# Softmax over 16,384 rows: tiles of twelve rows a partition in four buffers, instead of eight rows in six

## The chip, the cores and the metric

The kernel runs on one core of one Trainium2 chip. The metric is the device time of one execution in microseconds (us); for the kernel before it is the median of five runs. The engines named in the text are VectorE (DVE), ScalarE (ACT), SyncE (SP, which only issues loads here) and the core's 16 DMA engines, which move data between the chip's main memory (HBM) and the on-chip memory (SBUF, 128 partitions).

## The reference

A softmax with a temperature over the last axis of a 32 x 512 x 1024 array of float32 (64 MiB in, 64 MiB out):

```python
def reference(x, temperature):          # temperature = 0.5
    scaled = x / temperature
    shifted = scaled - np.max(scaled, axis=-1, keepdims=True)
    exp_x = np.exp(shifted)
    return (exp_x / np.sum(exp_x, axis=-1, keepdims=True)).astype(np.float32)
```

Each of the 16,384 rows of 1024 elements is independent of the others.

## The kernel before

The rows are cut into 16 tiles. A tile has eight neighbouring rows in each of 128 partitions, so a partition's share is 8 x 4 KiB = 32 KiB that lie in one piece in HBM and in SBUF, and the tile is 4 MiB. `TILES` (L10) lists the rows a partition of each tile, and `BUFS` (L11) says how many tiles' buffers there are: six, 192 KiB a partition. All work on a tile is done in place.

`load` (L57) issues one transfer of a whole tile on SP's queue. `store` (L97) issues one transfer of a whole tile on ACT's queue, and then calls `load` for the next tile that has not been loaded. That load goes into the buffer whose store was the oldest, and SP waits until that store has landed before it issues it (L61).

Inside a tile the rows are worked on in groups of four (`GROUP`, L13). For each group:

- `maximum` (L64): one VectorE reduction over 128 x 4 x 1024 elements (L70, the rows' maxima), and one tiny VectorE multiplication that makes the bias (L73).
- `exponential` (L75): four ScalarE activations (L79), one a row, which compute exp(scale * x + bias) in place and the row's sum beside it.
- `divide` (L88): one tiny VectorE reciprocal of the four sums (L91) and four VectorE multiplications (L93), one a row.

The order is written out by hand, with the scheduler of the language switched off. First `BUFS` loads are issued. Then a loop goes over the groups of all tiles; in each step comes the maximum and the exponential of group g, and then the division and the store of group g-1:

```python
for g in range(len(groups) + 1):
    if g < len(groups):
        maximum(g)
        exponential(g)
    if g > 0:
        divide(g - 1)
        store(g - 1)      # issues something only after a tile's last group
```

So the last division of a tile, and with it its store, stands on VectorE behind the first maximum of the next tile, which waits for that tile's load.

Of the kernel before, what the change touches and what calls it, by code (L numbers as in the profile page):

```python
# [1 line left out]

# [4 lines left out]

TILES = [[8]] * 16  # L10
BUFS = 6  # L11

GROUP = 4  # L13


@with_exitstack
def kernel(
    ctx: ExitStack,
    tc: tile.TileContext,
    x: bass.AP,  # L20
    temperature: bass.AP,
    out: bass.AP,
):
    nc = tc.nc
    f32 = mybir.dt.float32
    scale = 1.0 / float(temperature)
    extreme = mybir.AluOpType.max if scale > 0 else mybir.AluOpType.min

    P = 128
    xf = x.flatten_outer_dims()  # L30
    of = out.flatten_outer_dims()
    n, d = xf.shape
    assert sum(sum(ks) for ks in TILES) * P == n

    data = ctx.enter_context(tc.tile_pool(name="data", bufs=BUFS))
    stats = ctx.enter_context(tc.tile_pool(name="stats", bufs=4))


    groups, first, r = [], [], 0
    for i, ks in enumerate(TILES):  # L40
        first.append(r)
        r += sum(ks)
        a = 0
        for k in ks:
            for b in range(0, k, GROUP):
                m = min(GROUP, k - b)
                groups.append((i, a + b, m, (a, k) if b + m == k else None))
            a += k

    def dram(t, i):  # L50
        k = sum(TILES[i])
        block = t[P * first[i] : P * (first[i] + k), :]
        return block.rearrange("(p k) d -> p k d", p=P, k=k)

    tiles, small = [], []

    def load():  # L57
        i = len(tiles)
        if i < len(TILES):
            xt = data.tile([P, sum(TILES[i]), d], f32, name="xt")  # L60
            nc.sync.dma_start(out=xt, in_=dram(xf, i))  # L61
            tiles.append(xt)

    def maximum(g):  # L64
        i, a, k, _ = groups[g]
        top, bias, sums, recip = (
            stats.tile([P, k], f32, name=name) for name in ("top", "bias", "sums", "recip")
        )
        small.append((bias, sums, recip))
        nc.vector.tensor_reduce(  # L70
            out=top, in_=tiles[i][:, a : a + k, :], axis=mybir.AxisListType.X, op=extreme
        )
        nc.vector.tensor_scalar_mul(bias, in0=top, scalar1=-scale)  # L73

    def exponential(g):  # L75
        i, a, k, _ = groups[g]
        bias, sums, _ = small[g]
        for b in range(k):
            nc.scalar.activation(  # L79
                tiles[i][:, a + b, :],  # L80
                tiles[i][:, a + b, :],
                mybir.ActivationFunctionType.Exp,
                bias=bias[:, b : b + 1],
                scale=scale,
                accum_out=sums[:, b : b + 1],
            )

    def divide(g):  # L88
        i, a, k, _ = groups[g]
        _, sums, recip = small[g]  # L90
        nc.vector.reciprocal(recip, sums)  # L91
        for b in range(k):
            nc.vector.tensor_scalar_mul(  # L93
                tiles[i][:, a + b, :], in0=tiles[i][:, a + b, :], scalar1=recip[:, b : b + 1]
            )

    def store(g):  # L97
        i, _, _, part = groups[g]
        if part:
            a, k = part  # L100
            nc.scalar.dma_start(out=dram(of, i)[:, a : a + k, :], in_=tiles[i][:, a : a + k, :])
            if a + k == sum(TILES[i]):
                load()

    with tc.manual_schedule():
        for _ in range(BUFS):
            load()
# [6 lines that stand above are left out]
                store(g - 1)  # L116


# [1 line left out]
_INS = ['x', 'temperature']  # L120
_OUTS = [((32, 512, 1024), 'float32')]

_NUMBERS = {'temperature': 0.5}


# [26 lines left out]
```

## Time and profile before

| what | value |
|---|---|
| median of 5 runs | 318.04 us (317.62 to 318.44) |
| the profiled execution | 317.94 us |
| its span, first to last instruction | 316.1 us |
| VectorE busy | 235.5 us (75%) |
| ScalarE busy | 149.6 us (47%) |
| moved by DMA | 134.25 MB, 425 GB/s over the span |
| loads: 16 of 4096 KB | 50.1 us from issue to landing (median) |
| stores: 16 of 4096 KB | 38.7 us from issue to landing (median) |

The profile is of one execution. The span is what its trace covers; the time of the execution has 1.8 us more around it. A transfer's time to landing contains the time that it stands behind others in its queue. The share of the DMA engines is the mean over 16 engines.

### The profile page before, as it was taken

How to read it: one execution, taken by the hardware profiler on the slowest of the kernel's cores; microseconds unless marked ns; L12 is line 12 of the kernel's file. 1: busy time of each engine (PE TensorE's matmuls, PEld its weight loads, DVE VectorE, ACT ScalarE, POOL GpSimd, SP SyncE). 2: the span in 40 equal slices, each digit the busy share in tenths (PEclk: the TensorE clock that was granted, in tenths of full speed). 3: DMA queues.
4: the chain of work that ended last, by engine and by line, in shares of the span. 5: the costliest groups of instructions: out<-in, count | busy, mean ns of one | idle time of the engine just before them, and what ended most of it. 6: DMA issues, size and time to landing. Idle time of an engine off the chain costs nothing.

```text
span 316.1 us, 620 instructions
## 1 busy us (share of the span) xinstructions
DVE 235.5 (75%) x224; ACT 149.6 (47%) x257; POOL 0.2 (0%) x4
## 2 busy tenths in 40 slices
DVE  0399999999689494994949859497693976949720
ACT  0176666666526255361554606556064560645500
POOL 0000000000000000000000000000000000000000
DMA  8999999999999999999999999999999999999996
GB/s 332 398 464 415 382 460 423 440 429 435 444 419 448 415 452 411 452 415 452 411 452 411 453 423 444 427 435 444 419 448 416 448 415 448 415 452 411 452 411 274
DMA packets 4612, 134.25 MB, mean 425 GB/s; under 512 B 512, under 2 KB 512, under 8 KB 512
## 3 DMA queue, kind: packets, MB, share of 16 engines
q1 hardware_dynamic: 2304, 67.11, 49.6%
q10 hardware_dynamic: 2304, 67.11, 49.2%
q14 instruction: 4, 0.03, 0.0%
HBM read 67.11 MB, written 67.11 MB: 425 GB/s over the span
## 4 chain that ended last, share of the span: by engine, by line
DVE 49%; DMA 32%; another core or an unknown queue 9%; ACT 5%; issue 1%; DVEq 0%; SPq 0%
DVE top L70 29%; DMA xt<-in_x_dram 20%; DVE xt L93 18%; DMA out_dram<-xt 12%; ACT xt L79 5%; DVE recip L91 1%; DVE bias L73 1%; DVEq L147 0%; SPq L61 0%
## 5 line engine op out<-in xcount | busy, mean ns | idle before, releaser
L79 ACT ACTIVATE xt<-xt,bias 128x1024 f32<-128x1024 f32 x128 | 145.4, 1137 | 136.7 <-DVE recip L91 119.4
L70 DVE TENSOR_REDUCE top<-xt 128x4 f32<-128x4096 f32 x32 | 141.3, 4416 | 62.6 <-DMA xt<-in_x_dram 62.6
L93 DVE TENSOR_SCALAR xt<-xt,recip 128x1024 f32<-128x1024 f32 x128 | 87.7, 750 | 1.1
L79 ACT ACTIVATION_READ_ACCUMULATOR xt<-xt,bias 128x1 f32 x128 | 23.9, 186 | 0.0
L79 ACT ACT_TABLE_LOAD x1 | 1.3, 1283 | 13.1 <-DMA xt<-in_x_dram 13.1
L91 DVE RECIPROCAL recip<-sums 128x4 f32<-128x4 f32 x32 | 5.5, 171 | 2.1 <-ACT xt L79 2.1
L73 DVE TENSOR_SCALAR bias<-top 128x4 f32<-128x4 f32 x32 | 5.5, 170 | 1.1
L133 POOL MEMSET const-uint8-127<- 128x1 uint8 x1 | 0.1, 103 | 0.0
L133 POOL MEMSET const-bfloat16-1.0<- 128x1 bf16 x1 | 0.1, 102 | 0.0
L133 POOL MEMSET const-float32-0.0<- 128x1 f32 x1 | 0.1, 99 | 0.2 <-issue 0.2
L133 POOL MEMSET const-float32-1.0<- 128x1 f32 x1 | 0.1, 99 | 0.0
## 6 DMA issues: line engine op xcount, KB each, us to landing
xt<-in_x_dram SPq DMA_DIRECT2D x16, 4096.0 KB, 50.1
out_dram<-xt ACTq DMA_DIRECT2D x16, 4096.0 KB, 38.7
```

The lines of the kernel that those rows point to most:

```text
L70: nc.vector.tensor_reduce(out=top, in_=tiles[i][:, a : a + k, :], axis=mybir.AxisListType.X, op=extreme)
L73: nc.vector.tensor_scalar_mul(bias, in0=top, scalar1=-scale)
L79: nc.scalar.activation(tiles[i][:, a + b, :], tiles[i][:, a + b, :], mybir.ActivationFunctionType.Exp, bias=bias[:, b : b + 1], scale=scal ...
L91: nc.vector.reciprocal(recip, sums)
L93: nc.vector.tensor_scalar_mul(tiles[i][:, a + b, :], in0=tiles[i][:, a + b, :], scalar1=recip[:, b : b + 1])
L133: nc = _bacc.Bacc("TRN2", target_bir_lowering=False, num_devices=1)
```

## The change

Ten tiles of twelve rows a partition (48 KiB a partition, 6 MiB a tile) and one of eight rows (4 MiB) take the place of 16 tiles of eight rows, and four buffers take the place of six. A buffer has the size of the largest tile, so the buffers take 192 KiB a partition as before. The groups of four rows stay: a tile of twelve has three groups, the last tile two. The loop and the order in it are not touched.

```diff
-TILES = [[8]] * 16
-BUFS = 6
+TILES = [[12]] * 10 + [[8]]
+BUFS = 4
```

## The prediction

> **What bounds the kernel now.** I read the page's busy shares and slices first, then its queue lines, then the windows at the start, the middle and the end, then the waits, and last the timeline around the first and the last store. The page first:
>
> ```profile
> DVE 235.5 (75%) x224; ACT 149.6 (47%) x257; POOL 0.2 (0%) x4
> DMA  8999999999999999999999999999999999999996
> DMA packets 4612, 134.25 MB, mean 425 GB/s; under 512 B 512, under 2 KB 512, under 8 KB 512
> q1 hardware_dynamic: 2304, 67.11, 49.6%
> q10 hardware_dynamic: 2304, 67.11, 49.2%
> ```
>
> VectorE is idle a quarter of the span, ScalarE half; the DMA engines are full in every slice but the first and last. The two queues (q1 loads, q10 stores) together occupy 98.8% of 16 engines. Each has 2304 packets; 512 of all packets are tiny (one completion packet for each of 16 engines and 32 transfers), so 2048 of each queue are data: 67.11 MB / 2048 = 32,768 bytes, one partition's eight rows. The windows (start and end, then busy us with instructions of DVE, ACT, POOL, then clock, DMA share, GB/s) show where the engines are not full:
>
> ```profile
> 0.00:8.00 8.00, 0.00 (x0) 0.00 (x0) 0.20 (x4) 1.00 0.84 328
> 33.00:60.00 27.00, 26.72 (x25) 15.95 (x29) 0.00 (x0) 1.00 0.98 413
> 120.00:200.00 80.00, 61.22 (x60) 39.40 (x69) 0.00 (x0) 1.00 1.00 433
> 290.00:302.00 12.00, 9.99 (x13) 6.66 (x12) 0.00 (x0) 1.00 1.01 437
> 302.00:310.00 8.00, 0.41 (x1) 0.00 (x0) 0.00 (x0) 1.00 1.04 446
> 310.00:316.00 6.00, 0.00 (x0) 0.00 (x0) 0.00 (x0) 1.00 0.47 202
> ```
>
> Nothing is lost between about 2 us and 313 us, neither with loads alone (before 33 us), nor mixed, nor with stores alone. So the limit is the transfer work itself, and the waits agree: both computing engines and the load queue wait, in the end, for transfers.
>
> ```profile
> DVE top L70 <- DMA xt<-in_x_dram: 62.6, 12, 13.1
> SPq L61 <- DMA out_dram<-xt: 224.5, 10, 53.8
> ```
>
> The timeline gives the distances that decide whether the engines stay full (start, us, instruction):
>
> ```profile
> 13.07 4.42 DVE L70 TENSOR_REDUCE top<-xt 128x4 f32<-128x4096 f32 x1 [13.07 <-DMA xt<-in_x_dram]
> ...
> 32.78 0.38 ACTq L101 DMA_DIRECT2D out_dram<-xt  x1
> ...
> 282.68 4.42 DVE L70 TENSOR_REDUCE top<-xt 128x4 f32<-128x4096 f32 x1 [4.49 <-DMA xt<-in_x_dram]
> ...
> 290.19 0.34 ACTq L101 DMA_DIRECT2D out_dram<-xt  x1
> ...
> 302.44 0.34 ACTq L101 DMA_DIRECT2D out_dram<-xt  x1
> ```
>
> A tile's store leaves 7.5 us after the next tile lands (282.68 to 290.19), because its last division stands behind the next tile's first maximum; the last store leaves 19.8 us after the last landing. The packet records show the next-to-last store ending at 304.5 us and the last one's first packet at 303.3 us: the end is covered, by 1.2 us.
>
> **The change, part by part.** *Bytes* do not change: 134.2 MB. *Instructions* of VectorE and ScalarE do not change: 128 rows in groups of four are still 32 groups; of the issues, SP's and ACT's fall from 16 to 11 each. *Buffers*: 6 x 32 KiB and 4 x 48 KiB are both 192 KiB a partition.
>
> *Packets.* In the records a 32,768-byte packet starts 1,209.4 ns after the one before it, a 4-byte one 5.9 ns. (Two mixed rounds in the trace say the same: loads are seen to land 19.37 us apart, 204.58 to 223.95 on VectorE, and 16 x 1.209 + 2 x 0.006 = 19.36.) The line through the two has 27.22 bytes per ns and 5.7 ns for a packet as such. A 49,152-byte packet is then 1,805.7 + 5.7 = 1,811.4 ns. No row has that size, so two bounds: with no cost per packet it is 1.5 x 1,209.4 = 1,814.1 ns (saving nothing), and with all that the 4-byte packet shows, 1,811.2 ns. I take 1,811.4, since both rows lie on that line by construction and 4-byte packets are nearly all overhead.
> Per engine before: 16 tiles x 2 directions x 8 packets = 256 x 1.2094 + 32 x 0.006 = 309.80 us. After: 160 x 1.8114 + 16 x 1.2094 + 22 x 0.006 = 289.82 + 19.35 + 0.13 = 309.30 us. Saved: 0.5 us; bounds 0.1 (completion packets alone) and 0.5. Nothing in the trace excludes that a longer packet is slower per byte; that would be a loss, and the first rival prices its likeliest form.
> The Trainium skill, "DMA: Bandwidth & Descriptors", section "Why small descriptors are slow (HBM only)", gives a packet about 3 fixed cycles beside its 32-byte beats; by it a 32 KiB packet is 1024 + 3 cycles, and losing a third of them would be worth an estimated 0.3 us. The same page, section "SWDGE vs HWDGE vs iDMA", speaks against the change: a packet is the boundary at which an engine switches between queues, preferably at most 4096 bytes; here 32 KiB pieces already move as one packet at 433 GB/s in the mixed window, so no cost of it is seen.
>
> *Start.* The first transfer is half as long again: its first packet comes at 1.7 us as before, its landing at 13.05 + 8 x 0.602 = 17.9 us. The first store goes from after the second group to after the third: 32.78 - 13.05 = 19.7 us after landing, plus one group's step of 7.39 us (L70 starts at 32.66 and 40.05), so 45.0 us, 12.2 us later. The cover: 24 MiB of loads are in flight in both kernels, 4 x (8 x 1.811) = 58.0 us of work, ending alone at 60.5 us (0.75 us of first-packet latency included). By the packet records the first store's first packet came at 37.1 us, 4.3 us after its issue; again so, 49.3 us. 11.2 us of load work remains: covered, cost nothing. If that cover were gone, each us later would cost one.
>
> *Middle.* From 49.3 us both queues alternate. Loads end at 49.3 + 2 x 11.2 = 71.7; store 0 at 75.0, landing at 75.4 and releasing load 4 on SP, whose first packet (0.9 us after issue, as at 302.44) is at 76.4. For those 4.7 us no load is queued, but store 1 has been since 45.0 + 22.2 = 67.2 us. After that a load and a store of twelve rows take 29.0 us; load 4 lands near 105.8, load 9 at 250.8, VectorE needs 22.2 of each 29.0. Store to load release overlaps: store 1 lands at 103.0, the load before ends at 105.4.
>
> *End.* Load 10 is small: its eight 1.21 us packets alternate with 1.81 us ones, 24.2 us, landing at 275.0. Store 8 was issued at 250.8 + 7.5 = 258.3, store 9 at 282.5, store 10 at 275.0 + 19.8 = 294.8. Counted back from an end of work at 314.4 us: store 10 takes 9.7 us alone, store 9 14.5, so 9 begins near 290.2 and 10 near 304.7: each is queued some 8 to 10 us before its turn. No gap, cost nothing.
>
> *Sum.* The profiled execution took 317.94 us (span 316.1 and 1.8 around it), 0.1 under the median of 318.04. 317.94 - 0.5 = 317.44 (317.9 by the other bound), or 318.04 - 0.5 = 317.54 from the median; I take **317.5 us**.
>
> **The rivals.**
> *The pieces are cut.* If 48 KiB does not go as one packet, the change does not do what it says. As 32 + 16 KiB it is 16 packets a tile and direction: 336 an engine, 80 more than now, + 0.46 us: 318.4. As 16 KiB, 496: + 240 x 5.7 ns = 1.4, 319.3. Against: 32 KiB is seen whole. For: nothing larger is seen.
> *The shift at the start reaches the end (slower).* One mechanism: both rings run dry once because the first store is late, after which the 4.8 us later start is never caught up: 317.94 - 0.5 + 4.8 = 322.2. Place: between 45 and 76 us. It decides only if the first store's first packet comes after 60.5 us instead of 49.3; or if store 1 is issued after 75.0 instead of 67.2. For: the chain of waits of now begins with the landing and VectorE's unbroken work. Against: 62.6 us of VectorE's waiting for loads, which absorbs a late start.
> *The last engine.* By the records the engines' last packets end between 313.0 and 313.8 us, except two at 314.2 and 314.9, which each carried two instruction-fetch packets (8,192 bytes, 0.3 to 0.6 us of delay each). If those fall otherwise, up to 1.1 us more goes: 316.4.
>
> **How the numbers follow.** Forecast 0.68: its own range 316.9 to 318.1 (the saving between nothing and 0.5, and half a us either way for the last engine). What a measurement here can tell from no change is about 0.2%, 0.64 us, so faster means under 317.40: half of this case, 0.34 faster and 0.34 same. Last engine 0.11, faster. Cut pieces 0.07: 0.02 same, 0.05 slower. Shift 0.14, slower. Faster 0.45, same 0.36, slower 0.19. The range 316.4 to 319.0 takes in the forecast, the last engine and the milder cut, and leaves out the shift and the finer cuts, under 0.2.
>
> **What would show it.** Right: 1584 packets in each queue (11 transfers of 128 data and 16 completion packets), slices at 9 throughout, first store near 45 us, last near 295, DMA share of 0.99 or more in every window from 10 to 310 us. Wrong: more than 1584 packets in a queue (cut pieces); a window under 0.95 around 45 to 76 us or 280 to 305 us (shift, or an end that is not covered); a mixed rate under 430 GB/s, which no step here foresees.

## The result, and the profile after

The changed kernel takes **320.04 us** (median of 21 runs, 318.10 to 323.05); the kernel before took 318.01 us beside it (41 runs, 317.62 to 318.99). The ratio is 1.0055, 95% interval 1.0041 to 1.0069: slower by half a per cent, outside the forecast's range and on the other side of no change. As striking as the median is the spread: 5 us where the kernel before has 1.4. The ratios in this document leave out runs over 1.5% above the fastest of the same kernel, here the one of 323.05 us from which the first profile is, so for kernels with a wide spread they come out low. A second profile is read below, of a run of 319.96 us with a span of 317.9; the five runs taken with it were 319.96 to 320.81.

The page's slices and queue lines of that second profile:

```profile
DVE 235.1 (74%) x224; ACT 149.6 (47%) x257; POOL 0.2 (0%) x4
DMA  8999999999999999999999999999999999997997
DMA packets 3172, 134.25 MB, mean 422 GB/s; under 512 B 352, under 2 KB 352, under 8 KB 352
q1 hardware_dynamic: 1584, 67.11, 49.4%
q10 hardware_dynamic: 1584, 67.11, 48.8%
```

There are 1584 packets in each queue, as foreseen: the pieces are not cut. But with fewer packets and the same bytes, the two queues' share of a span that is 1.8 us longer has hardly fallen: 98.2% of 317.9 is 312.2 us, where 98.8% of 316.1 was 312.3. The work that should have become 0.5 us less did not. And a slice near the end shows a 7. The windows (start and end, busy us with instructions of DVE, ACT, POOL, clock, DMA share, GB/s):

```profile
33.00:60.00 27.00, 26.72 (x28) 16.36 (x29) 0.00 (x0) 1.00 1.02 433
60.00:90.00 30.00, 29.72 (x30) 19.01 (x33) 0.00 (x0) 1.00 0.98 422
120.00:200.00 80.00, 58.78 (x57) 39.02 (x68) 0.00 (x0) 1.00 1.00 432
282.00:290.00 8.00, 6.20 (x6) 2.89 (x7) 0.00 (x0) 1.00 0.77 332
290.00:302.00 12.00, 9.99 (x12) 7.71 (x14) 0.00 (x0) 1.00 0.92 397
302.00:310.00 8.00, 1.46 (x3) 0.00 (x0) 0.00 (x0) 1.00 0.91 393
```

The mixed middle runs at 432 GB/s, as before; then engines stand idle from 282 to 310 us, where the forecast had every transfer queued 8 to 10 us ahead. Two of the signs that it named for being wrong are here: an end that is not covered (0.77 and 0.92) and a mixed rate under 430 GB/s (422 from 60 to 90 us). The share needs care, since the kernel before has a window under 0.95 in the same place, although no engine has a gap there in its records:

```profile
282.00:290.00 8.00, 7.25 (x7) 2.61 (x5) 0.00 (x0) 1.00 0.94 406
```

The timeline (start, us, instruction; the issues of loads 4 and 5 are merged into one line) shows the late landing behind it:

```profile
45.57 0.38 ACTq L101 DMA_DIRECT2D out_dram<-xt  x1
...
78.26 25.66 SPq L61 DMA_DIRECT2D xt<-in_x_dram  x2
...
283.73 4.42 DVE L70 TENSOR_REDUCE top<-xt 128x4 f32<-128x4096 f32 x1 [2.28 <-DMA xt<-in_x_dram]
...
291.24 0.34 ACTq L101 DMA_DIRECT2D out_dram<-xt  x1
...
303.49 0.34 ACTq L101 DMA_DIRECT2D out_dram<-xt  x1
```

The last load landed at 283.7 instead of 275.0, so store 9 left at 291.2 instead of 282.5. The packet records say why. Of the 16 engines, 14 had finished their share of that load between 277.4 and 278.5 us; the last two at 280.8 and 281.6. The Trainium skill, "DMA: Bandwidth & Descriptors", section "Why a DMA increments its semaphore by 16 and not by 1", says that only the full count of all engines tells of a landing; this trace agrees, with the landing behind the last engine: its data ended at 281.6, its completion packet came behind one more store packet, at 283.4, and VectorE started at 283.7. Twelve engines ended store 8 near 288.5 and then stood idle for 3.2 to 3.9 us.

What delays an engine can be summed from the records. They do not name the engine; a packet is given to the engine whose packet before it ends as it starts, and the number of packets that each engine has of each transfer decides between several. The sums are good to some 0.3 us, and whether it is the same engine in every run is not known. A 32 KiB packet usually takes 1,213 ns, one of 48 KiB 1,815 (packets overlap by 3 to 4 ns, which gives the steps of 1,209 and 1,812). Call what a packet takes beyond the usual time of its length a *stall*, and sum stalls over each engine, without its first packet:

```
stalls per engine, us       largest   second   median engine
before                        1.7       1.5        0.7
changed, first profile        7.0       5.4        0.8
changed, second profile       4.0       3.3        0.8
```

The median engine is as it was. Single engines are not. Their stalls are nearly all on load packets, up to 1.1 us each, they are other sums in each run, and they set in at 48 us, when the first store's packets come between the loads.

These sums give the times. In all three profiles the engine that ends last has no gap, or 0.2 us of one, between its first packet and its last, while the others of the changed kernel stand idle for up to 3.9 us (second profile) and 6.8 us (first). So its own work is what the kernel takes. With 0.5 us less of packets the second profile should be 4.0 - 1.7 - 0.5 = 1.8 us longer than the one before, and the first 7.0 - 1.7 - 0.5 = 4.8; the spans are 1.8 and 4.9 us longer (317.9 and 321.0 against 316.1).

Instruction fetches alone do not explain a late engine. The two late engines of the second profile and the latest of the first each carried two of them (0.3 us each), but the second engine of the first profile (5.4 us) carried none, nor did the latest with the tiles in another order (4.7) and with short exponentials (8.6), two runs further down.

### The profile page after: what moved, and what is told of

It is laid out like the page before. It is cut to its first block, busy times and chain, and to the rows that moved or that the text cites. A ratio compares the mean times of both kernels' runs of the same rounds, so it can differ in the third digit from the quotient of the medians.

```text
span 321.0 us, 600 instructions
## 1 busy us (share of the span) xinstructions
DVE 235.1 (73%) x224; ACT 149.6 (47%) x257; POOL 0.2 (0%) x4
## 3 DMA queue, kind: packets, MB, share of 16 engines
q1 hardware_dynamic: 1584, 67.11, 48.9%
q10 hardware_dynamic: 1584, 67.11, 48.4%
## 4 chain that ended last, share of the span: by engine, by line
DMA 65%; DVE 23%; ACT 6%; issue 1%; DVEq 0%; SPq 0%
DMA xt<-in_x_dram 41%; DMA out_dram<-xt 24%; DVE top L70 15%; DVE xt L93 7%; ACT xt L79 6%; DVE bias L73 0%; DVE recip L91 0%; DVEq L147 0%; SPq L61 0%
## 5 line engine op out<-in xcount | busy, mean ns | idle before, releaser
L79 ACT ACTIVATE xt<-xt,bias 128x1024 f32<-128x1024 f32 x128 | 145.4, 1137 | 135.4 <-DVE recip L91 120.8
L79 ACT ACTIVATION_READ_ACCUMULATOR xt<-xt,bias 128x1 f32 x128 | 23.9, 186 | 0.0
```

Of the source, the lines that this page charges most:

```text
L79: nc.scalar.activation(tiles[i][:, a + b, :], tiles[i][:, a + b, :], mybir.ActivationFunctionType.Exp, bias=bias[:, b : b + 1], scale=scal ...
```

## The experiments

Three theories to begin with: *long packets* stall; a *step* of 48 KiB in the address from partition to partition makes engines collide; or the stalls were always there, and *fewer transfers* in fewer buffers no longer absorb them. All kernels below are edits of the changed kernel; each ratio is to the kernel before, run on the same chip.

**The changed kernel again** (no edit).

> The changed kernel once more, for a second profile. In the first one 14 of the 16 DMA engines followed the forecast (their share of the last load ended at 273.7 to 274.3 us) and two did not (281.2 and 284.3 us), because packets of 1.81 us took up to 1.6 us longer on those two, mostly loads. Three theories for these stalls. Long packets: pieces of 48 KiB stall where 32 KiB do not. Address step: a step of 48 KiB from partition to partition makes engines collide in the memory where 32 KiB does not. Fewer transfers: the stalls are always there, but with 11 transfers in four buffers each landing waits for the slowest engine and nothing absorbs it. All three: about 320 us, spread over 318 to 323; the time follows the slowest engine's sum of stalls, 1 us of it at 318.3 and 5 us at 322. Only fewer transfers: stalls no larger than the 2 us of the kernel before.

320.10 us (319.96 to 320.81), ratio 1.0073 (1.0061 to 1.0086). Stalls of 4.0 and 3.3 us on two engines, against 1.7 before: the stalls are larger than before, not only less well absorbed.

**Pieces cut in half, everything else kept.**

```diff
-            nc.sync.dma_start(out=xt, in_=dram(xf, i))
+            h = sum(TILES[i]) // 2
+            for b in (h, 0):
+                nc.sync.dma_start(out=xt[:, b : b + h, :], in_=dram(xf, i)[:, b : b + h, :])
...
-            nc.scalar.dma_start(out=dram(of, i)[:, a : a + k, :], in_=tiles[i][:, a : a + k, :])
+            h = k // 2
+            for b in (a, a + h):
+                nc.scalar.dma_start(out=dram(of, i)[:, b : b + h, :], in_=tiles[i][:, b : b + h, :])
```

> Each tile is loaded and stored in two transfers of half its rows (24 KiB pieces at a step of 48 KiB; the second half is loaded first, so that the first group still waits for the whole tile). Tiles, buffers and order as in the changed kernel; 336 packets an engine, some 0.9 us of packet cost more than with 171. Long packets: stalls gone, 318.4 (318.0 to 318.9), spread under 1 us. Address step and fewer transfers: 319.5 to 321, spread of 3 us or more, one or two engines with 3 to 6 us of stalls.

318.86 us (318.70 to 319.02), ratio 1.0027 (1.0016 to 1.0037). The spread falls to 0.3 us and the largest stall sum to 2.0. The same tiles, buffers, order and address step, so neither the step nor the tile size makes the stalls. The last tile is cut too, which makes 352 packets an engine instead of the 336 expected. The remaining 0.9 us over the kernel before is more than the 0.5 that 96 more packets cost; the rest was not taken apart.

**Tiles of six rows in eight buffers** (`TILES = [[6]] * 21 + [[2]]`, `BUFS = 8`).

> 21 tiles of six rows and one of two, in eight buffers (192 KiB as before): pieces of 24 KiB at a step of 24 KiB, which like 48 KiB is no power of two. 344 packets an engine, 0.5 us of packet cost more than the kernel before. Long packets and fewer transfers: 318.5 (318.1 to 319.0), little spread. Address step: stalls on single engines, 319.5 to 321, spread of 3 us.

318.51 us (318.37 to 318.86), ratio 1.0018 (1.0009 to 1.0027); largest stall sum 1.9. The forecast's price of a packet holds here: 96 more of them than in the kernel before (352, not the 344 expected), at 5.7 ns + 0.5 us, and 0.5 us measured.

**The kernel before with five buffers** (`TILES = [[8]] * 16`, `BUFS = 5`).

> The kernel before with five buffers instead of six (160 KiB): one transfer less in reserve, pieces of 32 KiB as before. Long packets and address step: 317.8 to 318.4, the same as before, since the load queue of the kernel before has 19 us in reserve and loses one tile of it. Fewer transfers: slower and spread, 318.8 to 320.

317.85 us (317.69 to 318.40), ratio 0.9996 (0.9988 to 1.0005): no difference. A transfer less in reserve costs nothing while no engine is late.

Long packets are left. The next runs ask how a late engine turns into time, and which packets must be long.

**Store 9 no longer waits for load 10.**

```diff
         for g in range(len(groups) + 1):
+            early = g == len(groups) - 2
+            if early:
+                divide(g - 1)
+                store(g - 1)
             if g < len(groups):
                 maximum(g)
                 exponential(g)
-            if g > 0:
+            if g > 0 and not early:
```

> The changed kernel with one thing moved: ahead of the last tile's first maximum come the last division and the store of the tile before it, so that store 9 no longer waits for the landing of load 10. In the second profile of the changed kernel 12 of 16 DMA engines stood idle for 3.2 to 3.9 us from 288.4 us on, since store 9 was issued 7.5 us after load 10 had landed, and that landing waited for the engines with stalls; those engines themselves stood idle for 0.4 to 1.1 us only. Stalls and late store together: the gap closes, and the slowest engine's own work is left: 318.9 (318.3 to 319.5). Stalls alone: 320.1, unchanged. Late store alone: 317.3.

319.48 us (318.14 to 321.91), ratio 1.0052 (1.0028 to 1.0077): not to be told from the changed kernel. Its profile, of a run of 318.15 us, shows store 9 at 284.45 and the end filled (timeline, then windows):

```profile
284.45 0.34 ACTq L101 DMA_DIRECT2D out_dram<-xt  x1
```

```profile
282.00:290.00 8.00, 7.96 (x7) 0.96 (x1) 0.00 (x0) 1.00 0.98 424
290.00:302.00 12.00, 9.28 (x12) 8.21 (x16) 0.00 (x0) 1.00 1.02 442
```

But the spread of the times stays. The profiled run is one of the three fastest of the twelve, with a largest stall sum of 2.9 us; no longer run of this kernel was profiled. In the changed kernel the idle time at the end was that of engines that waited for the late ones. How much of the median the gap itself costs is not settled: the last store still waits for the last landing, and the expected 318.9 lies within what was seen.

**Ten rows, and ten rows with the same move** (`TILES = [[10]] * 12 + [[8]]`; the second with the edit above).

> Twelve tiles of ten rows and one of eight in four buffers: 40 KiB pieces, 208 packets an engine, 0.3 us of packet cost less than the kernel before. If stalls grow with the length of a piece: one or two engines with 2 to 4 us, 318.6 (318.0 to 319.3). If they begin only above 40 KiB: 317.7 (317.4 to 318.1). If they begin right above 32 KiB: 319 to 320.5 as with twelve rows.

> Tiles of ten rows, with the store of the last large tile moved ahead of the last tile's first maximum. With ten rows no engine had stalls over 2 us, but engines stood idle for 1 to 1.8 us from 291.3 us on, waiting for the store that followed the last landing. If that late store is the whole loss of ten rows: 317.2 (316.9 to 317.7), the packet saving of 0.3 us and a little more, faster than both kernels. If a kernel of this length ends with its transfer work anyway, the gap only moves: 318.3, unchanged.

318.34 us (318.21 to 318.83), ratio 1.0010 (1.0001 to 1.0019); with the move 318.42 (318.05 to 318.63), ratio 1.0010 (1.0002 to 1.0019). Both were to be faster than this by one theory or another. (The groups in a tile of ten are of four, four and two rows, which gives VectorE 242 instructions instead of 224.) The windows of the two profiles, without and with the move:

```profile
290.00:302.00 12.00, 9.92 (x14) 9.28 (x16) 0.00 (x0) 1.00 0.85 365
```

```profile
290.00:302.00 12.00, 10.09 (x12) 9.10 (x16) 0.00 (x0) 1.00 0.99 427
```

The move fills the end (0.85 to 0.99) and the time stays: in the first the engines all end at 314.9 to 315.0 us, in the second between 313.0 and 315.1. The slowest engine sets the end, and a gap on the others costs nothing: without the move two engines had no gap at all. At 40 KiB the largest stall sums are 2.3 and 2.5 us, each on an engine that carried two instruction fetches, and the eleven times of each kernel lie within 0.7 us.

**Eleven rows** (`TILES = [[11]] * 11 + [[7]]`, 44 KiB).

> Eleven tiles of eleven rows and one of seven in four buffers: 44 KiB pieces, 190 packets an engine. Ten rows took 318.2 to 318.8 without single engines behind, twelve rows 318.1 to 323. If the stalls grow with length: 318.9 (318.3 to 319.6), with a spread of 1 to 2 us. If something is special at 48 KiB: 318.2 (317.9 to 318.6), spread under 1 us.

319.31 us (317.69 to 324.59), ratio 1.0034 (1.0009 to 1.0058): a spread of 7 us, stalls of 4.3 and 3.4 us. So 48 KiB is not special, and the effect is hardly gradual: between 40 and 44 KiB the spread goes from 0.6 us to 7.

**Only the stores cut, and only the loads cut** (one half of the edit of the halves each).

> Only the stores are cut into two transfers of six rows (24 KiB pieces); loads stay at 48 KiB. 264 packets an engine. Packet for packet the loads then move twice the bytes of the stores, so the loads run ahead and the last one lands some 10 us earlier: no gap at the end. If long load pieces stall by themselves: single engines with 2 to 7 us of load stalls as before, 318.9 (318.3 to 319.8). If a long load stalls only beside a long store: stalls under 2 us on every engine, 318.1 (317.8 to 318.5).

> Only the loads are cut into two transfers of six rows (24 KiB pieces), the stores stay at 48 KiB: the reverse of half_stores, which had no engine behind. Packet for packet the stores then move twice the bytes of the loads, the last load lands late and the end is not covered: by the distances of the trace some 320.7 us, for this reason alone. What counts is the stalls: if a long piece on either side is enough, single engines have more than 3 us; if both sides must be long, none over 2.5 us and a narrow spread.

With short stores beside loads of 48 KiB: 318.41 us (317.97 to 318.72), ratio 1.0009 (1.0000 to 1.0018), largest stall sum 2.2. With stores of 48 KiB beside short loads: **338.83 us** (336.68 to 340.18), ratio 1.0645 (1.0616 to 1.0674). The windows, first with short stores, then with short loads:

```profile
100.00:200.00 100.00, 79.31 (x78) 50.69 (x87) 0.00 (x0) 1.00 1.00 431
```

```profile
100.00:200.00 100.00, 68.64 (x68) 42.62 (x73) 0.00 (x0) 1.00 1.01 421
300.00:320.00 20.00, 14.73 (x14) 9.10 (x16) 0.00 (x0) 1.00 0.47 202
```

In the second kernel the engines are just as full in the middle (1.01) and move less (421 GB/s): packets take longer. Every engine has stalls now, 15.5 us on the worst and 6.6 on the median one, on loads of 24 KiB and on stores alike. On top of that the end is uncovered (0.47 from 300 to 320 us), and that is the larger part of the 20.8 us: the median engine stands idle for some 18 us in sum, 13 of them in one piece from 298.6 us on, where the expectation came to 320.7 us for the uncovered end alone. At 48 KiB, long loads beside short stores do not stall; the stalls come with the long *stores*, though on the median engine it is mostly the loads between them that are seen to take longer. Both edits change the rhythm too, since between 100 and 200 us the queue with the short pieces now runs alone for stretches; so the length of the stores is not wholly separated from it.

**The tiles in another order**, so that the distance in memory between the two streams changes.

```diff
+    first[:10] = [first[j] for j in (0, 5, 1, 6, 2, 7, 3, 8, 4, 9)]
```

> The changed kernel, with its ten large tiles taken in the order 0 5 1 6 2 7 3 8 4 9 of the array, so that the distance in memory between what is being loaded and what is being stored changes from tile to tile. If stalls come from 48 KiB pieces as such: 320 (319.3 to 320.8), spread from 318 to 322. If they come from the fixed distance between the two streams: 317.5 to 318.6 with a narrow spread.

320.90 us (318.77 to 323.81), ratio 1.0083 (1.0050 to 1.0117), stalls up to 4.7 us: a fixed distance is not the cause.

**Transfers alone.** The loop calls only `store(g)`, and tiles are loaded and stored again. Twelve rows first in a single run and then in eleven, then the same with eight rows in six buffers:

```diff
             if g < len(groups):
-                maximum(g)
-                exponential(g)
-            if g > 0:
-                divide(g - 1)
-                store(g - 1)
+                store(g)
```

> All computation is left out: the tiles of twelve rows are loaded and stored again in four buffers, so that only the transfers are left, and the output is the input. If the stalls are the DMA engines' own: single engines with 2 us or more of load stalls. If they come from VectorE's and ScalarE's accesses to the same memory: none over 1.5 us. The time itself is the transfer work and the first landing, about 317 us, and a little more with stalls.

> The transfers of the changed kernel without any computation (the output is the input), now timed. The single look gave 317.37 us with no engine far behind, but so did single runs of the changed kernel (318.1). If the stalls are the DMA engines' own, the times are spread as in the changed kernel: 317.3 to 321, median 318.5 or more. If they need the computing engines beside them: 317.2 to 317.8, spread as narrow as that of the kernel before.

> The same for the kernel before: tiles of eight rows in six buffers, loads and stores alone, the output is the input. By packets it has 0.5 us more work than with twelve rows: 317.8 (317.4 to 318.3) in every theory, with a spread under 1 us. If copying twelve rows is faster than this by 0.4 to 0.5 us, the saving of the forecast is real, and what hides it is the stalls.

The single run with twelve rows took 317.37 us, the eleven 317.34 (317.09 to 319.17); with eight rows 316.71 (316.64 to 317.01). Ten of the eleven runs with twelve rows lie under 318.0, so without computation the long pieces hardly lag. And yet twelve rows are 0.6 us *slower* here. The median engine stalls for 1.3 us in sum with twelve rows and 0.8 with eight, most of it where the first stores come between the loads; its last packet ends at 313.4 and 313.3 us. On the median engine the half microsecond saved on packets is lost again at that one place. The last engine ends at 314.2 and 313.9 us; the rest of the 0.6 us was not taken apart.

**Whose work beside the transfers brings the stalls out?** The exponentials, VectorE's passes, or both cut to 8 of a row's 1024 elements; and the copy of twelve rows with VectorE busy on a scratch tile of its own. Shown is VectorE's part; ScalarE's activations (L79) are cut to `0:8` in the same way, and the edit with the scratch tile is not shown.

```diff
-            out=top, in_=tiles[i][:, a : a + k, :], axis=mybir.AxisListType.X, op=extreme
+            out=top, in_=tiles[i][:, a : a + k, 0:8], axis=mybir.AxisListType.X, op=extreme
...
-                tiles[i][:, a + b, :], in0=tiles[i][:, a + b, :], scalar1=recip[:, b : b + 1]
+                tiles[i][:, a + b, 0:8], in0=tiles[i][:, a + b, 0:8], scalar1=recip[:, b : b + 1]
```

> The changed kernel, with ScalarE's exponentials cut to 8 of a row's 1024 elements (the output is not the softmax). VectorE and all transfers are as in the changed kernel, and so is the time of the first store within 5 us. Copying alone took 317.1 to 319.2 us with twelve rows, the full kernel 318.1 to 323. If ScalarE's traffic in the on-chip memory makes the stalls: 317.3 (317.0 to 318.0), narrow. If VectorE's, or only the timing of the stores: 319.3 to 320.5, spread from 318 to 322.

> The changed kernel, with VectorE's maxima and divisions cut to 8 of 1024 elements of a row, ScalarE in full (the output is not the softmax). A tile then takes ScalarE some 14 us instead of VectorE's 22. If VectorE's traffic makes the stalls: 317.3 (317.0 to 318.0), narrow. If ScalarE's: 319.3 to 320.5, spread.

> Both cut to 8 of 1024 elements: every instruction, wait and issue is there, with hardly any traffic (the output is not the softmax). If the engines' traffic makes the stalls: 317.3 (317.0 to 318.0). If the waits and the order of issues make them: 319 to 320.5, spread.

> The copy of twelve-row tiles without any computation on them, and beside it VectorE with the full kernel's load of maxima and multiplications, 32 groups on an 8 KiB scratch tile that no transfer touches and that waits for none (the output is the input). Transfers and their rhythm are those of copy12. If VectorE's traffic in the on-chip memory makes the stalls: spread, 318 to 321, median 318.5 or more. If it is the rhythm of loads and stores in the full kernel: 317.3 (317.0 to 317.9), as copy12.

Short exponentials: 321.03 us (317.54 to 324.56), ratio 1.0049 (1.0020 to 1.0078), by the medians 1.0094, spread like the full kernel; ScalarE's traffic is not needed. Short work on VectorE: 318.33 (318.19 to 320.66), eleven of twelve runs under 318.6. Both short: 318.79 (318.46 to 321.59), three of ten runs at 319.9 or more. The copy with VectorE busy beside it: 318.15 (317.95 to 318.56), with no engine behind but one, which carried two instruction fetches (2.6 us of stalls in sum). That engine ends last, at 315.1 us where the copy ends at 314.2, and the copy alone is 0.8 us faster. VectorE's work there runs without a pause and is over at some 233 us, on memory that no transfer touches. So VectorE's traffic of that kind does not make the stalls, and taking nearly all traffic away does not quite end them. One candidate left is the rhythm in which loads and stores follow each other, which VectorE's time sets; no run isolates it, and it stays open why long stores stall here and not in the copy.

## Why the prediction was wrong

*The start* was late by 0.6 us and otherwise right: first landing 18.5 us (17.9 said), first store 45.6 (45.0).

*The packet's own time* was right: 1,811.4 ns worked out, steps of 1,812 ns in the records. Its worth was not: the sum of 309.3 against 309.8 us holds only for an engine without stalls, and the copies show that the first mixing of loads and stores takes 0.5 us back even on the median engine. Two figures beside it were off without bearing on the outcome. The last store of the kernel before was queued with next to nothing in hand, not 1.2 us ahead: each engine starts it as it ends the store before, between 303.3 and 305.2 us, and 303.3 is 0.9 us after its issue. And by its own terms (317.9 and half a us) the forecast's range reaches to 318.4, not 318.1.

*The middle* had one term too small: load 4 was given 0.9 us from issue to first packet, like the last store's. It stood at an empty queue beside a busy one, as store 0 had in the kernel before, and took 4.4 us like that one (78.3 to 82.7 us). It lost 2.8 us more because store 0's landing waited for the slowest engine (78.2 instead of 75.4). That used up part of the cover at the end.

*The step that failed* is in the sum, where the stalls of before were kept for the last engine ("half a us either way for the last engine"). The stalls of the slowest engine, the term behind it, grew from 1.7 us to 4.0 in the second profile and 7.0 in the first, which is 2.3 and 5.3 us instead of half a us; together with the 0.5 us saved this is the difference of the spans. The sentence ahead of it, that nothing excludes a longer packet being slower per byte, named the opening; but it priced only cut pieces, and as a uniform cost of all engines. The longer pieces did not make packets slower on the median engine (0.7 and 0.8 us of stalls); they made single engines late, by other sums in each run, and a transfer lands with its last engine.

*The end*: on 14 engines the last load was done at 277.4 to 278.5 us, 3 to 4 us after the 274.6 worked out, because of load 4; with its landing there, store 9 would have left near 288 us, about when these engines ended store 8 (288.3 to 288.9). The two late engines took the rest. In the first profile most engines met the forecast (273.7 to 274.3 us), but by chance: load 4 was as late there (82.6 us), and store 8 left 3.0 us later than in the second (269.7 against 266.7), which left the last load alone in the queues for longer. *The rival of the shift* had the right sign and the wrong place: the two queues did not run dry together at 45 to 76 us (share 1.02 and 0.98 in the windows); the load queue alone stood empty until 82.7 us. *The rival of the last engine* looked at the right quantity and only at what could be gained from it.

*The rule that spoke against the change*, in the Trainium skill, "DMA: Bandwidth & Descriptors", section "SWDGE vs HWDGE vs iDMA", wants packets of at most 4096 bytes preferably, in a table on what GpSimd builds, while SP and ACT issue the transfers here. No run has pieces that short, so the limit itself is not tested; from 24 to 40 KiB the kernels lie within 0.3% of each other. Its direction was right above 40 KiB, and the forecast dismissed it on a row of 32 KiB.

No version that computes the softmax beats the kernel before. Five buffers (0.9996) equal it with 32 KiB less memory.

## What to carry to other kernels

When the DMA engines are full from end to end, the time is that of the slowest of them (spans 1.8 and 4.9 us longer in the two profiles here), so look at each engine's last packet and not only at the mean share; an average of 0.98 can hide two engines that hold up fourteen. Closing a gap on engines that wait for a late one gained nothing here (318.34 and 318.42 us with ten rows). Pieces larger than those a trace already shows working are a cost that the trace cannot bound: test stores and loads apart, since here cutting the stores ended the stalls and cutting the loads did not.

## What the runs showed of the hardware that was not expected

- In this softmax, stores in pieces of 44 or 48 KiB beside loads as long make single DMA engines late: largest stall sums of 2.9 to 7.0 us in the five profiles, and times spread over 4 to 7 us. With pieces of up to 40 KiB on both sides the sums are 2.5 us at most and the spread under 1.4. Loads of 48 KiB beside stores of 24 KiB do not (2.2 us), nor do both at 48 KiB without computation (2.5 and 1.8 us).
- Stores of 48 KiB beside loads of 24 KiB: 338.8 us, some 18 us of idle time on the median engine, most of it at the end, and 6.6 us of stalls.
- A transfer that joins an empty queue while the other queue is busy has its first packet 3.5 to 4.9 us after its issue, over eight of the profiles, with pieces of 24, 32 and 48 KiB; one that finds both queues all but empty, 0.8 to 1.0 us.
